# Program order for TensorE in the expert stage, merged slot products, and unread products between trunk and experts

## The chip, the cores and the metric

The kernel runs on one core of a Trainium2 chip. The metric is device time in microseconds (us) of one execution; the time of a kernel is the median of its runs. One execution was taken by the hardware profiler as well. The engines are named as in its rows: PE is TensorE (PEld its weight loads), DVE is VectorE, ACT is ScalarE, POOL is GpSimd, SP is SyncE, which issues most of the DMA transfers.

## The reference

A decoder of two layers over 512 tokens of width 1024, in fp32. Each layer has two attention branches, gates, an output projection, and a feed-forward part: dense in layer 0, and in layer 1 the mixture of experts, at which the change is aimed:

```python
D_MODEL, SEQ, DEPTH = 1024, 512, 2
N_EXPERTS, TOP_K, D_FF_EXPERT = 8, 2, 1408

def swiglu(h, w_gu, w_dn):
    gu = h @ w_gu
    g, u = jnp.split(gu, 2, axis=-1)
    return (jax.nn.silu(g) * u) @ w_dn

def moe_swiglu(h, w_router, w_gu_e, w_dn_e):
    """Top-2 of 8 SwiGLU experts; softmax over the selected router logits."""
    logits = (h @ w_router).astype(jnp.float32)
    top_val, top_idx = lax.top_k(logits, TOP_K)
    top_w = jax.nn.softmax(top_val, axis=-1)
    combine = jnp.sum(jax.nn.one_hot(top_idx, N_EXPERTS, dtype=jnp.float32) * top_w[..., None], axis=-2)
    combine = combine.astype(h.dtype)
    out = jnp.zeros_like(h)
    for e in range(N_EXPERTS):
        out = out + combine[..., e:e + 1] * swiglu(h, w_gu_e[e], w_dn_e[e])
    return out

def reference(...):
    for l in range(DEPTH):
        ...                                  # attention branches, gates
        x = x + (g_sb * y_sb + g_fx * y_fx) @ w_out[l]
        h = rmsnorm(x, g_ffn[l])
        if l % 2 == 0:
            x = x + swiglu(h, w_gu_dense[l // 2], w_dn_dense[l // 2])
        else:
            x = x + moe_swiglu(h, w_router[l // 2], w_gu_exp[l // 2], w_dn_exp[l // 2])
    return x
```

## The kernel before, in words

**Numbers.** An fp32 operand is split into a high part of type fp32r (a cast) and a low part (a subtraction), and a product of two operands is the sum of three products on PE: high by high, high by low, low by high. The weights of the experts come from memory as fp32 (`er`, by SP's queue, eleven raw buffers) and are split in the kernel: ACT makes `ehi` (L1467), DVE makes `elo` (L1468). `e_split` (L1455) does this for one piece, two pieces ahead of the product that reads it; the table `SN` says at which steps.

**From trunk to experts.** The last projection of the trunk (`out_proj1`, L1041) makes, half by half, the router logits (`half_logits`, L1070) and the two best experts of each token (`top2`, L1162). `route` (L1174) turns the choice into positions: where in its expert's list a token stands (products with triangular matrices, on PE). `moe` (L1705) then prepares the first expert. `prep_a` (L1485) compares the positions with a row of numbers (`one_hots`, L1268, tiles `oh`), multiplies the one-hots with token numbers (`slots`, L1278: 16 products of one column for 192 slots in two groups), casts the sums to an index `ix`, and issues the gather of the tokens' rows by POOL (an indirect DMA, 128 rows to `xg`, and under an If 64 more rows to a part of `ao`). The routing weights of the slots come from `slot_weights` (L1298, 8 products of three columns). `prep_b` (L1517) transposes the gathered rows on PE (L1526) and splits them into `xh` and `xl`; `prep_over` (L1532) does the same for the 64 further rows, into `aot`.

**An expert.** `expert_blocks` (L1551) has four gate/up blocks u of 352 + 352 columns, each of k = 0..7 with six products of 352 columns (L1646 gate, L1647 up), and then three blocks of the down projection with k = 0..10 and three products each (L1680 to L1682). A step is named (u, k); the down projection's are (4, k) to (6, k). After each block the result is activated (`am`), transposed, and split into `ah` and `al` (`tr`, L1567, L1581). Experts with more than 128 tokens (in these inputs the first and the fifth) run the further 64 rows as well: products under an If at the start of each block (L1626, over-products, into the two PSUM banks `mm`), folded by `ov_gu` (L1585: ACT copies, DVE adds, ACT's silu, DVE multiplies; `fold` is L1546), transposed by `ov_tr` (L1592, L1597, L1601), and multiplied with the down weights (L1694, L1695). The next expert is prepared meanwhile: `prep_a` at the steps `PA`, `PA1`, `PA2`, `prep_b` at `PB`, `PB1`, `prep_over` at `PO`; the rest of the first expert's preparation (`route_rest`, L1206: weights and a ranking of the experts by their counts) at `P0`. `OV`, `OV3` and `OT` are the k at which the folding and `ov_tr` stand.

**What sets the order.** ACT's instructions stand in the order in which the code issues them. Those of PE, DVE and POOL are put in order by a scheduler, by estimates and dependences, except where the code calls `keep_in_program_order`. In the trunk this holds for PE as well.

## Time and profile before

| | before |
|---|---|
| median of 3 runs | 1703.38 us (1703.5, 1700.21, 1703.38) |
| profiled execution | 1699.52 us |
| its span, first to last instruction | 1697.7 us |
| mean granted clock of PE | 0.992 |
| PE busy | 1634.0 us, 96% of the span |
| DVE / ACT / POOL busy | 64% / 58% / 12% |
| moved by DMA | 273.73 MB, 161 GB/s on average |

A row of the windows gives the busy time of each engine in a stretch, its number of instructions in brackets, the clock granted to PE as a share of full speed, the mean busy share of the 16 DMA engines, and what they moved. A row of the timeline gives the start, the busy time, engine, source line, operation, output and inputs by the program's names, the shape, and how many such instructions the row joins; in square brackets stand the idle time of the engine ahead of it and what released it. Ends of products are modelled and a product's row is longer than the distance to the next one, so the distance from start to start is what a product costs in a dense row of them. The trunk fills the span up to some 1183 us, the first expert's products begin at 1198.00 us, and the eighth expert ends at some 1685 us.

### The profile page before, as it was taken

How to read it: one execution, taken by the hardware profiler on the slowest of the kernel's cores; microseconds unless marked ns; L12 is line 12 of the kernel's file. 1: busy time of each engine (PE TensorE's matmuls, PEld its weight loads, DVE VectorE, ACT ScalarE, POOL GpSimd, SP SyncE). 2: the span in 40 equal slices, each digit the busy share in tenths (PEclk: the TensorE clock that was granted, in tenths of full speed). 3: DMA queues.
4: the chain of work that ended last, by engine and by line, in shares of the span. 5: the costliest groups of instructions: out<-in, count | busy, mean ns of one | idle time of the engine just before them, and what ended most of it. 6: DMA issues, size and time to landing. Idle time of an engine off the chain costs nothing. (4 is left out here: it accounts for less than half of the span.)

```text
span 1697.7 us, 26160 instructions
## 1 busy us (share of the span) xinstructions
PE 1634.0 (96%) x9031; PEld 1425.7 (84%) x9031; DVE 1093.7 (64%) x1844; ACT 977.9 (58%) x1750; POOL 205.5 (12%) x315
## 2 busy tenths in 40 slices
PE   6999999999999999999999999998899999999996
PEld 6878987888888888888878987887889999999996
DVE  5588678666533332336588688655767878767984
ACT  5677589755322222324677589643656776656873
POOL 6122000001000000100122000102012201102200
PEclk9999999999999999999999999999899999999998
DMA  7334332235333332443433233352959899869993
GB/s 181 108 96 116 82 88 71 86 110 165 100 98 99 100 99 84 134 130 100 112 105 107 72 88 78 110 194 95 311 201 331 296 360 351 295 209 336 321 344 87
DMA packets 270840, 273.73 MB, mean 161 GB/s; under 512 B 11424, under 2 KB 259232, under 8 KB 270688
## 3 DMA queue, kind: packets, MB, share of 16 engines
q1 hardware_dynamic: 255936, 230.98, 43.2%
q0 software_dynamic: 12288, 37.40, 8.1%
q10 hardware_dynamic: 2464, 3.41, 0.6%
q8 instruction: 85, 1.39, 0.3%
q14 instruction: 67, 0.55, 0.1%
HBM read 250.21 MB, written 13.14 MB: 155 GB/s over the span
## 5 line engine op out<-in xcount | busy, mean ns | idle before, releaser
L320 PE MATMUL mm<-b,whi 128*128 128x512 f32 x1072 | 426.7, 398 | 3.6 <-DVE b L534 2.7
L322 PE MATMUL mm<-b,wlo 128*128 128x512 f32 x1072 | 419.4, 391 | 0.0
L321 PE MATMUL mm<-b,whi 128*128 128x512 f32 x1072 | 419.4, 391 | 0.0
L297 DVE TENSOR_TENSOR wlo<-wr,whi 128x1024 fp32r<-128x1024 f32 (+1 forms) x176 | 213.3, 1213 | 214.5 <-ACT whi L296 212.5
L296 ACT CAST whi<-wr 128x1024 fp32r<-128x1024 f32 (+1 forms) x176 | 183.2, 1043 | 268.9 <-PE mm L321 121.5
L1468 DVE TENSOR_TENSOR elo<-er,ehi 128x1408 fp32r<-128x1408 f32 (+3 forms) x200 | 305.1, 1569 | 26.0 <-ACT ehi L1467 15.9
L1467 ACT CAST ehi<-er 128x1408 fp32r<-128x1408 f32 (+3 forms) x200 | 256.2, 1324 | 18.7 <-DMA er<-in_w_gu_exp_dram 6.2
L320 PEld LDWEIGHTS mm<-b,whi 128*128 128x128 f32 x1072 | 201.7, 188 | 45.4 <-DVE b L534 4.7
L322 PEld LDWEIGHTS mm<-b,wlo 128*128 128x128 f32 x1072 | 201.3, 188 | 42.8 <-DVE wlo L297 0.4
L321 PEld LDWEIGHTS mm<-b,whi 128*128 128x128 f32 x1072 | 201.7, 188 | 38.5 <-issue 0.2
L356 PE MATMUL mm<-whi,b 128*128 128x256 f32 x320 | 92.0, 288 | 1.8 <-DVE b L532 1.1
L357 PE MATMUL mm<-wlo,b 128*128 128x256 f32 x320 | 91.0, 285 | 0.4 <-DVE wlo L297 0.4
L358 PE MATMUL mm<-whi,b 128*128 128x256 f32 x320 | 90.8, 284 | 0.0
L1681 PE MATMUL pa<-elo,ah 128*128 128x352 f32 (+1 forms) x264 | 85.6, 324 | 2.7
L1682 PE MATMUL pa<-ehi,al 128*128 128x352 f32 (+1 forms) x264 | 84.4, 320 | 3.3 <-DVE al L1581 3.3
L1680 PE MATMUL pa<-ehi,ah 128*128 128x352 f32 (+1 forms) x264 | 86.2, 327 | 0.9
L1647 PE MATMUL pa<-elo,xh 128*128 128x352 f32 x256 | 83.7, 327 | 2.1 <-PEq L1620 0.5
L1646 PE MATMUL pa<-ehi,xh 128*128 128x352 f32 x256 | 85.7, 335 | 0.0
L1647 PE MATMUL pa<-ehi,xl 128*128 128x352 f32 x256 | 83.2, 325 | 0.9
L1646 PE MATMUL pa<-elo,xh 128*128 128x352 f32 x256 | 83.0, 324 | 0.3 <-DVE elo L1468 0.3
L1646 PE MATMUL pa<-ehi,xl 128*128 128x352 f32 x256 | 83.2, 325 | 0.0
L1647 PE MATMUL pa<-ehi,xh 128*128 128x352 f32 x256 | 82.9, 324 | 0.0
(351 smaller groups left out, 3087.7 us busy)
## 6 DMA issues: line engine op xcount, KB each, us to landing
er<-in_w_gu_exp_dram SPq DMA_DIRECT2D x248, 352.0 KB
wr<-in_w_in_dram SPq DMA_DIRECT2D x80, 512.0 KB
wr<-in_w_gu_dense_dram SPq DMA_DIRECT2D x44, 512.0 KB
er<-in_w_dn_exp_dram SPq DMA_DIRECT2D x32, 704.0 KB
wr<-in_w_dn_dense_dram SPq DMA_DIRECT2D x20, 512.0 KB
er<-in_w_dn_exp_dram SPq DMA_DIRECT2D x16, 640.0 KB
er<-in_w_dn_exp_dram SPq DMA_DIRECT2D x16, 528.0 KB
b<-b POOLq DMA_DIRECT2D x64, 128.0 KB, 2.8
```

Of the source, the lines that this page charges most:

```text
L296: self.nc.scalar.copy(hi, raw)
L297: self.nc.vector.tensor_sub(lo, raw, f32v(hi))
L320: self.nc.tensor.matmul(ps, hi[:, j], hh[j], start=st, stop=False)
L321: self.nc.tensor.matmul(ps, hi[:, j], hl[j], start=False, stop=False)
L322: self.nc.tensor.matmul(ps, lo[:, j], hh[j], start=False, stop=sp)
L356: nc.tensor.matmul(o, a, hi[:, j], start=first, stop=False, skip_group_check=True)
L357: nc.tensor.matmul(o, a, lo[:, j], start=False, stop=False, skip_group_check=True)
L358: nc.tensor.matmul(o, b, hi[:, j], start=False, stop=last, skip_group_check=True)
L1467: self.nc.scalar.copy(hi, raw)
L1468: self.last_dve = self.nc.vector.tensor_sub(lo, raw, f32v(hi))
L1646: nc.tensor.matmul(pg, x[:, k], w[:, 0, kk], start=s0, stop=s1)
L1647: nc.tensor.matmul(pu, x[:, k], w[:, 1, kk], start=s0, stop=s1)
```

## The change

- **Order on PE.** The call of `moe` stands in a context that keeps PE's instructions in program order, too. With it go changes of place: the over-products of a block (`mm_over`) are issued at the block's start, but for the first block of the first expert, where `prep_over` is issued at k = 2 and the over-products at k = 4; the folding `ov_gu` stands at k = 5 of each block (k = 7 in the first block of the first expert), that of the last gate/up block too, and `ov_tr` at k = 3 of the down projection, not 8.
- **Preparation.** `PA` becomes (2, 1), (2, 6), (3, 1) while the first expert runs, and (0, 6), (1, 5), (2, 4) in the others. `route_rest` is issued ahead of the first expert's blocks, its slot weights at the new `P0`, (2, 0) and (2, 2). The one-hots are all made on DVE.
- **Slot products.** In the seven later experts `slots_all` multiplies the one-hots with five columns at once: three of the weight and two of the token number, which POOL copies into `cols`. Eight products take the place of 16 and 8, and two sums on DVE take the place of a cast and a sum per group.
- **Unread products.** `busy(n)` issues n bf16 products of 384 columns, of constants, into a PSUM tile that nothing reads: 3 and 13 around the last logits, 4 in `route`, 28 after the first expert's slot products.

```diff
--- before.py
+++ after.py
@@ -44,14 +44,16 @@
 ER = 11
 EA = 4
 ORDER = (7, 3, 4, 5, 0, 6, 1, 2)
-P0 = (0, 2), (0, 6), (1, 1)
-OV, OV3, OT, OY = 5, 6, 8, (5, 8)
+P0 = (2, 0), (2, 2)
+EO = 2
+OV, OT, OY = 5, 3, (5, 8)
 ER0 = 3
 LA = 2
 SN = (2, 4, 6, 8), (2, 4, 6, 8), (2, 4, 6, 8), (2, 4, 6), (7, 8, 9, 10), (1, 4, 8), (1, 4, 8)
 TU, TE = 5, 6
 TD = 5
-PA, PA1, PA2, PB, PB1, PO = (1, 2), (2, 0), (2, 4), (4, 2), (4, 7), (5, 4)
+PA = ((2, 1), (2, 6), (3, 1)), ((0, 6), (1, 5), (2, 4))
+PB, PB1, PO = (4, 2), (4, 7), (5, 4)
 FD = 3
 PINH = ()
 BK = 0, 1, 2, 3, 4, 5, 6, 7
@@ -1081,6 +1083,9 @@
             if after:
                 after()
             yield
+            last = t == NT - 1 and c == 1
+            if last:
+                self.busy(3)
             for j in range(4):
                 q = slice(j * P, (j + 1) * P)
                 if t == NT - 1:
@@ -1090,6 +1095,8 @@
                     nc.tensor.matmul(pl[:64, t * P:(t + 1) * P], self.wr[:, 4 * c + j], p[:, q],
                                      start=t + c + j == 0 and p is xs[0], stop=c + j == 4 and p is xs[1],
                                      skip_group_check=True)
+            if last:
+                self.busy(13)
 
         def ev_b(t, ps):
             v = x[t][1]
@@ -1138,6 +1145,13 @@
                 yield
 
         self.run(self.proj_tok(2, mh, ml, ev_a), second_half())
+
+    def busy(self, n):
+
+        ps = self.psa()
+        v, w = self.ident.bitcast(BF16)[:, :P], self.iotas.bitcast(BF16)
+        for _ in range(n):
+            self.tc.keep_in_program_order(self.nc.tensor.matmul(ps[:, :2 * CAP], v, w, start=True, stop=True))
 
     def router_consts(self):
         nc, cp, q = self.nc, self.cp, self.nc.gpsimd
@@ -1189,6 +1203,7 @@
                              stop=j == 1, skip_group_check=True)
         for t in range(NT):
             nc.tensor.matmul(pc[:, 0:NE], self.onesb, mb[:, t * NE:(t + 1) * NE], start=t == 0, stop=t == NT - 1)
+        self.busy(4)
         a, b = rp.tile([P, NT, NE], F32, name="r_a"), rp.tile([P, NT, NE], F32, name="r_b")
         nc.vector.tensor_scalar(b, self.M, -1.0, 1.0, op0=ALU.mult, op1=ALU.add)
         nc.vector.tensor_mul(a, pr[:, 0:32].rearrange("p (t e) -> p t e", e=NE), self.M)
@@ -1221,7 +1236,9 @@
         nc.vector.tensor_tensor(self.M, self.M, over_e(e2), op=ALU.mult)
         nc.vector.tensor_add(self.wt, self.s1, self.M)
         self.rank()
-        self.cols = rp.tile([P, NT, NE, 3], BF16, name="cols")
+        self.cols = rp.tile([P, NT, NE, 5], BF16, name="cols")
+        for j in range(2):
+            nc.gpsimd.tensor_copy(self.cols[:, :, :, 3 + j], self.tokc[:, :, j:j + 1].to_broadcast([P, NT, NE]))
         self.weight_cols(self.cols, self.wtr, rp.tile([P, NT, NE], F32, name="wrem"))
 
     def rank(self):
@@ -1275,6 +1292,26 @@
             oh.append(o)
         return oh
 
+    def slots_all(self, n, oh, cols):
+
+        nc, ps, res = self.nc, self.psy(), []
+        for b in range(0, n, P):
+            m = min(P, n - b)
+            o = ps[:m, (b // P) * 8:(b // P) * 8 + 5]
+            for t in range(NT):
+                nc.tensor.matmul(o, oh[t][:, b:b + m], cols[:, t], start=t == 0, stop=t == NT - 1)
+            res.append([b, m] + [self.ex.tile([P, 1], d, tag=g, bufs=4, name=self.nm(g))[:m]
+                                 for d, g in ((I32, "ix"), (F32, "w"))])
+
+        def fin():
+            for b, m, ix, w in res:
+                o = ps[:m, (b // P) * 8:(b // P) * 8 + 5]
+                with nc.allow_low_precision(reason="whole numbers below 512"):
+                    nc.vector.tensor_reduce(ix, o[:, 3:5], axis=AX.X, op=ALU.add)
+                nc.vector.tensor_reduce(w, o[:, 0:3], axis=AX.X, op=ALU.add)
+
+        return res, fin
+
     def slots(self, n, oh):
 
         nc = self.nc
@@ -1486,12 +1523,11 @@
 
         nc, ex = self.nc, self.ex
         o = ORDER[e]
-        oh = self.one_hots(CAP, self.posr[:, :, o:o + 1] if e else self.pos[:, :, 0:1], nc.gpsimd if e else nc.vector)
+        oh = self.one_hots(CAP, self.posr[:, :, o:o + 1] if e else self.pos[:, :, 0:1], nc.vector)
         yield
-        sl, fin = self.slots(CAP, oh)
+        sl, fin = self.slots_all(CAP, oh, self.cols[:, :, o]) if e else self.slots(CAP, oh)
         self.sl = sl
         if e:
-            wfin = self.slot_weights(oh, sl, self.cols[:, :, o], self.psl)
             yield
         fin()
         g = self.g = [ex.tile([P, D], F32, tag="xg0", bufs=1, name=self.nm("xg")), self.views[-1]]
@@ -1510,9 +1546,9 @@
             yield
             self.route_rest()
             yield
-            wfin = self.slot_weights(oh, sl, self.cols[:, :, o])
-            yield
-        wfin()
+            wfin = self.slot_weights(oh, sl, self.cols[:, :, o, 0:3])
+            yield
+            wfin()
 
     def prep_b(self):
 
@@ -1605,18 +1641,7 @@
             self.fold(yo[:, c], ops[d][:, :c.stop - c.start], yo[:, c])
             nc.vector.tensor_scalar_mul(yo[:, c], yo[:, c], sl[1][3])
 
-        def evac_gu(u, pg, pu):
-            c = slice(u * GC, (u + 1) * GC)
-            nc.scalar.activation(a[:, c], pg, AF.Silu)
-            nc.vector.tensor_mul(a[:, c], a[:, c], pu)
-
-        def evac_y(d, py):
-            c = dcol(d)
-            nc.scalar.activation(y[:, c], py, AF.Copy, scale=sl[0][3])
-
-        last = None
-        for u in range(DFE // GC):
-            ws = self.e_next(KD // GK)
+        def mm_over():
             with self.over(e):
                 for k in range(KD):
                     hi, lo = ws[k // GK]
@@ -1624,14 +1649,34 @@
                     for w, s0, s1 in ((hi, st, False), (lo, False, sp)):
                         for g in range(2):
                             nc.tensor.matmul(og[g], xo[:, k], w[:, g, kk], start=s0, stop=s1)
+
+        def evac_gu(u, pg, pu):
+            c = slice(u * GC, (u + 1) * GC)
+            nc.scalar.activation(a[:, c], pg, AF.Silu)
+            nc.vector.tensor_mul(a[:, c], a[:, c], pu)
+
+        def evac_y(d, py):
+            c = dcol(d)
+            nc.scalar.activation(y[:, c], py, AF.Copy, scale=sl[0][3])
+
+        last = None
+        for u in range(DFE // GC):
+            ws = self.e_next(KD // GK)
+            if (e, u) != (0, 0):
+                mm_over()
             if u:
                 evac_gu(u - 1, *last)
             last = pg, pu = self.psa()[:, :GC], self.psa()[:, :GC]
             for k in range(KD):
                 yield u, k
+                if (e, u, k) == (0, 0, EO):
+                    xo = self.prep_over(0)
+                    self.e_splits(LA)
+                if (e, u, k) == (0, 0, EO + 2):
+                    mm_over()
                 if (u, k) == (0, ER0) and self.rest:
                     self.rest()
-                if k == OV and u < 3:
+                if k == (OV if e or u else KD - 1):
                     with self.over(e):
                         ov_gu(u)
                 if k == TU:
@@ -1660,9 +1705,6 @@
                     tr(KE)()
                 if k in SN[4 + d]:
                     self.e_split()
-                if d == 0 and k == OV3:
-                    with self.over(e):
-                        ov_gu(3)
                 if d == 0 and k == OT:
                     with self.over(e):
                         ov_tr()
@@ -1714,6 +1756,7 @@
         pa = self.prep_a(0)
         next(pa)
         next(pa)
+        self.busy(28)
         self.hold = True
         self.e_splits(3)
         pb = self.prep_b()
@@ -1725,18 +1768,21 @@
             self.e_load()
         self.hold = False
         next(pb)
-        xo = self.prep_over(0)
-        self.e_splits(1 + LA)
+        xo = None
+        self.e_splits(1)
+        next(pa)
+        p0 = pa
         for e in range(NE):
             sl = self.sl
             for u, k in self.expert_blocks(e, sl, self.xs, xo):
                 if e == 0 and (u, k) in P0:
-                    next(pa, None)
+                    next(p0, None)
                 if e + 1 == NE:
                     continue
-                if (u, k) == PA:
+                at = PA[min(e, 1)]
+                if (u, k) == at[0]:
                     pa = self.prep_a(e + 1)
-                if (u, k) in (PA, PA1, PA2):
+                if (u, k) in at:
                     next(pa, None)
                 if (u, k) == PB:
                     pb = self.prep_b()
@@ -1848,7 +1894,8 @@
                 self.route()
             with experts:
                 self.moe_pools(experts)
-                self.moe()
+                with tc.manual_schedule(engines={mybir.EngineType.PE}):
+                    self.moe()
                 with tc.issue_after(self.last_dve.ins):
                     self.overflow_list()
         with ExitStack() as experts:
```

The first of two places: PE in the first expert. `pa` are the banks of the main products, `mm` those of the over-products, `xh`/`xl` the gathered rows and `ehi`/`elo` the split weights; the rows stand in the middle of the second gate/up block before.

```order
L1646 MATMUL pa_12002<-ehi_11893,xl_11726 128x352
L1647 MATMUL pa_12003<-ehi_11893,xl_11726 128x352
L1646 MATMUL pa_12002<-ehi_11893,xh_11725 128x352
L1647 MATMUL pa_12003<-ehi_11893,xh_11725 128x352
L1646 MATMUL pa_12002<-elo_11894,xh_11725 128x352
L1620 COMPARE_AND_BRANCH
L1626 MATMUL mm_11660<-ehi_11790,aot 128x352
L1626 MATMUL mm_11661<-ehi_11790,aot 128x352
L1626 MATMUL mm_11660<-elo_11791,aot 128x352
```

The over-products (L1626) of block 1 come behind 33 of the 48 main products of the block, the last five of which are shown. After the change PE has this, at the end of block 0 and the start of block 1 (L1680 is the If of the folding, L1691 and L1692 are the main products, L1645 is the If of the over-products):

```order
L1680 COMPARE_AND_BRANCH
L1680 UNCONDITIONAL_BRANCH x2
L1691 MATMUL pa_11874<-ehi_11825,xh_11779 128x352
L1692 MATMUL pa_11875<-ehi_11825,xh_11779 128x352
L1691 MATMUL pa_11874<-elo_11826,xh_11779 128x352
L1692 MATMUL pa_11875<-elo_11826,xh_11779 128x352
L1691 MATMUL pa_11874<-ehi_11825,xl_11780 128x352
L1692 MATMUL pa_11875<-ehi_11825,xl_11780 128x352
L1645 COMPARE_AND_BRANCH
L1651 MATMUL mm_11685<-ehi_11903,aot 128x352
L1651 MATMUL mm_11686<-ehi_11903,aot 128x352
```

The over-products (L1651) moved to the head of the block, six main products behind the branch of the folding; the main products of block 1 now stand behind them.

The second place: DVE in the first expert's down projection before. The three rows between the branches fold the last over-block, `al` is the low part of the activations, `aot` that of the further rows.

```order
L1664 COMPARE_AND_BRANCH
L1549 TENSOR_TENSOR ao<-mm_11660,ao 64x352
L1549 TENSOR_TENSOR ao<-mm_11661,ao 64x352
L1590 TENSOR_TENSOR ao<-ao 64x352
L1664 UNCONDITIONAL_BRANCH x2
L1581 TENSOR_TENSOR al_11802<-py_12424,ah_11801 128x384
L1529 TENSOR_TENSOR xl_12407<-py_12443,xh_12406 128x512
L1667 COMPARE_AND_BRANCH
L1601 TENSOR_TENSOR aot<-py_12468,aot 128x8x64
L1601 TENSOR_TENSOR aot<-py_12479,aot 128x3x64
```

After the change, the folding of the last over-block (L1585, L1626) and what follows it:

```order
L1680 COMPARE_AND_BRANCH
L1585 TENSOR_TENSOR ao<-mm_11685,ao 64x352
L1585 TENSOR_TENSOR ao<-mm_11686,ao 64x352
L1626 TENSOR_TENSOR ao<-ao 64x352
L1680 UNCONDITIONAL_BRANCH x2
L1505 TENSOR_TENSOR elo_12427<-er_12063,ehi_12426 128x1408
L1617 TENSOR_TENSOR al_11873<-py_12413,ah_11872 128x384
L1656 TENSOR_TENSOR am<-am,pa_12339 128x352
L1565 TENSOR_TENSOR xl_12454<-py_12455,xh_12453 128x512
L1709 COMPARE_AND_BRANCH
L1637 TENSOR_TENSOR aot<-py_12466,aot 128x8x64
L1637 TENSOR_TENSOR aot<-py_12477,aot 128x3x64
```

The folding moved ahead of a split of weights (`elo`) and of both subtractions into `al`, and the two rows for `aot` ahead of the second of these.

## Rows read from the trace of the kernel before

**Rows 1.** The page's head; busy us, share of the span, instructions.

```profile
span 1697.7 us, 26160 instructions
...
PE 1634.0 (96%) x9031; PEld 1425.7 (84%) x9031; DVE 1093.7 (64%) x1844; ACT 977.9 (58%) x1750; POOL 205.5 (12%) x315
```

**Rows 2.** Windows: the stretch, its length, and the columns named above.

```profile
1184.00:1186.00 2.00, 0.96 (x8) 0.89 (x9) 1.21 (x7) 0.50 (x2) 0.00 (x0) 1.00 0.41 154
1186.00:1188.00 2.00, 0.26 (x5) 0.19 (x5) 1.99 (x12) 0.00 (x0) 1.00 (x2) 0.70 0.23 90
1192.00:1194.00 2.00, 0.00 (x0) 0.00 (x0) 2.00 (x2) 1.65 (x2) 1.63 (x2) 0.50 0.63 178
1202.00:1204.00 2.00, 2.00 (x9) 2.00 (x9) 1.42 (x2) 2.00 (x2) 0.00 (x0) 0.53 1.04 347
1204.00:1206.00 2.00, 2.00 (x14) 2.00 (x14) 2.00 (x2) 1.53 (x2) 0.00 (x0) 1.00 1.04 366
1350.00:1400.00 50.00, 48.64 (x320) 46.64 (x320) 41.19 (x39) 36.07 (x38) 7.28 (x6) 1.00 1.05 354
```

**Rows 3.** Timeline between trunk and first expert, DVE and PE.

```profile
1188.87 0.99 DVE L1273 TENSOR_SCALAR oh<-iotas,r_pos 128x192 bf16<-128x192 f32 x4
...
1189.22 1.41 PE L1288 MATMUL py<-tokc,oh 128*128 128x1 bf16 x16 [0.89 <-DVE oh L1273]
...
1196.21 1.97 PE L1526 MATMUL py<-ident,xg 128*128 128x128 f32 x8 [5.58 <-DMA xg<-hd,ix]
...
1198.00 0.66 PE L1646 MATMUL pa<-ehi,xh 128*128 128x352 f32 x1
...
1198.75 0.50 PE L1646 MATMUL pa<-elo,xh 128*128 128x352 f32 x1
...
1199.04 0.50 PE L1647 MATMUL pa<-elo,xh 128*128 128x352 f32 x1
...
1200.27 1.08 PE L1539 MATMUL py<-ident,ao 64*128 64x64 f32 x8 [0.73 <-DMA ao<-hd,ix]
...
1201.28 0.66 PE L1646 MATMUL pa<-ehi,xl 128*128 128x352 f32 x1
...
1203.80 0.36 PE L1646 MATMUL pa<-ehi,xh 128*128 128x352 f32 x1
```

**Rows 4.** Timeline of PE in the second expert, where the third is prepared.

```profile
1306.31 0.32 PE L1647 MATMUL pa<-ehi,xl 128*128 128x352 f32 x1
1306.47 0.69 PE L1288 MATMUL py<-tokc,oh 128*128 128x1 bf16 x16
1307.10 0.47 PE L1306 MATMUL py<-cols,oh 128*128 128x3 bf16 x8
1307.50 0.43 PE L1646 MATMUL pa<-ehi,xh 128*128 128x352 f32 x1
```

**Rows 5.** Timeline of PE: down projection of the first and the fifth expert.

```profile
1265.49 0.43 PE L1682 MATMUL pa<-ehi,al 128*128 128x352 f32 x1 [2.11 <-DVE al L1581]
...
1268.84 0.40 PE L1694 MATMUL mm<-ehi,aot 128*128 128x352 f32 x1 [0.95 <-DVE aot L1601]
...
1506.89 0.43 PE L1682 MATMUL pa<-ehi,al 128*128 128x352 f32 x1 [1.15 <-DVE al L1581]
...
1510.10 0.40 PE L1694 MATMUL mm<-ehi,aot 128*128 128x352 f32 x1 [0.79 <-DVE aot L1601]
```

**Rows 6.** Timeline of the first expert's first block, ACT and DVE.

```profile
1207.02 1.38 ACT L1467 CAST ehi<-er 128x1408 fp32r<-128x1408 f32 x1 [0.56 <-DMA er<-in_w_gu_exp_dram]
...
1208.99 1.38 ACT L1467 CAST ehi<-er 128x1408 fp32r<-128x1408 f32 x1 [0.59 <-DMA er<-in_w_gu_exp_dram]
...
1211.22 0.93 ACT L1548 COPY ao<-mm 64x352 f32<-64x352 f32 x2 [0.85 <-PE mm L1626]
...
1211.70 1.07 DVE L1549 TENSOR_TENSOR ao<-mm,ao 64x352 f32<-64x352 f32 x2 [1.43 <-ACT ao L1548]
```

**Rows 7.** Waits of PE from 1183 us: what, total us, times, longest.

```profile
PE py L1288 <- POOL oh L1273: 0.7, 2, 0.5
```

More of the change, by code (lines that the diff above doesn't have):

```diff
@@ L1606, in ov_y @@
             nc.vector.tensor_scalar_mul(yo[:, c], yo[:, c], sl[1][3])
+        def mm_over():
+            with self.over(e):
+                for k in range(KD):
+                    hi, lo = ws[k // GK]
+                    st, sp, kk = k == 0, k == KD - 1, k % GK
+                    for w, s0, s1 in ((hi, st, False), (lo, False, sp)):
+                        for g in range(2):
+                            nc.tensor.matmul(og[g], xo[:, k], w[:, g, kk], start=s0, stop=s1)
         def evac_gu(u, pg, pu):
@@ L1619, in expert_blocks @@
             ws = self.e_next(KD // GK)
-            with self.over(e):
-                for k in range(KD):
-                    hi, lo = ws[k // GK]
-                    st, sp, kk = k == 0, k == KD - 1, k % GK
-                    for w, s0, s1 in ((hi, st, False), (lo, False, sp)):
-                        for g in range(2):
-                            nc.tensor.matmul(og[g], xo[:, k], w[:, g, kk], start=s0, stop=s1)
+            if (e, u) != (0, 0):
+                mm_over()
             if u:
@@ L1662, in expert_blocks @@
                     self.e_split()
-                if d == 0 and k == OV3:
-                    with self.over(e):
-                        ov_gu(3)
                 if d == 0 and k == OT:
```

## The prediction

> **What bounds the kernel now.** I read the page first, then the stretches of equal length, then the timeline of the two stretches in which TensorE (PE) is not busy, then who waits for whom. The page shows PE busy for 96% of a span of 1697.7 us [rows 1], so only PE's own time and the holes in it count. The execution took 1699.52 us, 1.8 us more than its span; the median of the three runs is 1703.38, 3.9 above it, so I make the sum against the profiled execution and take it off the median.
>
> The first hole lies between the trunk and the first expert. PE is busy 0.96 and 0.26 of 2 us, and then the granted clock goes to 0.50, the 1.2 GHz level; it is back at 1.00 (2.4 GHz) only after some 1203.8, by which time the first expert has long begun [rows 2]. In the hole stand the slot products, a gather for which PE waits 5.58 us, eight transposes, and then twelve products of the first expert at a pitch of 0.29 us [rows 3], where a steady expert has 0.16 (the 1306.31 and 1306.47 rows of [rows 4]). Among them PE waits once more for the second gather, the rows beyond 128 (L1539).
>
> The experts themselves are dense. What the change touches there is the slot products, 24 in 1.03 us of a steady expert [rows 4], and four waits in the two experts with more than 128 tokens, the first and the fifth: PE waits for al and aot there [rows 5]. DVE is busy 41.2 of 50 us in steady experts and PE 48.6 [rows 2].
>
> **The change part by part.**
>
> *Unread products.* 48 products of 384 columns are added. At the high level one costs 384/352 of 0.16, 0.175 us. The three and the thirteen stand where PE waits for the last logits and for r_Mb, the four where it waits for the one-hots (0.89 us idle, [rows 3]); 13 x 0.175 = 2.3 us fits into the holes of the 1184 and 1186 rows of [rows 2], which leave 1.04 and 1.74 us, with little to spare. The 28 take 4.9 us and begin after the slot products, at about 1190.9, so they end near 1195.8; the gathered rows come at 1196.2, or a quarter us earlier (below). If they run over, the transposes wait: between 0 and 0.5 us, I take 0. What they can buy is the clock of the work behind them. Twelve first products took 3.85 us (four from 1198.00 to 0.29 behind 1199.04, eight from 1201.28 to 1203.80) and would take 1.92: 1.9 us. Four of the eight transposes stand before the first cast: 1.97/4, 0.5 us, less 0.05. The eight transposes of the second gather, 1.01 us from row to row, halve: 0.45. The sixteen slot products, 1.41 us, take 0.63 at the high level [rows 4], but the last one-hot ends at 1189.86 [rows 3], so only 0.25 is left. The wait for the second gather shrinks by 0.2, since twelve products stand before it now, not four. Together 3.25 us, if the clock holds.
>
> *Program order, the first block of the first expert.* Now the over-products of block 1 stand at its start and not in its middle, and the folding of block 0 (ov_gu, which reads the same two PSUM banks) only six products ahead of them; behind the waiting product all of PE is queued. PE would be there at 1197.3 + 80 x 0.16 + 0.75 for the gather + 0.55 for its transposes = 1211.4. On ACT the folding stands behind the split of the ninth piece of weights. The pieces come 2.0 us apart (the splits at 1207.02 and 1208.99 each waited for a DMA, [rows 6]), so the ninth comes at about 1211.0; the loads wait for the first cast, which is 0.7 earlier now, so 1210.3. The split takes 1.38, and from the start of ACT's two copies to the end of DVE's two adds it is 1.55 [rows 6]: the banks are free at 1213.2, or at 1212.7 for the first. PE waits 1.6 us here, a new wait that eats half of the 3.25. Its bounds are 0 (the piece comes two us sooner) and 3.25. I take 1.6: **1.65 us** are left.
>
> *Merged slot products.* Per prepared expert sixteen one-column products (0.63 us, 1306.47 to 1307.10) go and eight of three columns become eight of five. The eight cost 0.40 in [rows 4]; two columns more are nothing at that pitch. Seven experts are prepared this way: 7 x 0.63 = **4.4 us**. On DVE the sums take the place of two casts; the one-hots (0.99 us for four, [rows 3]) come from POOL to DVE, whose 8.8 idle us of 50 hide them. The lower bound of a saved product is the 0.03 to which the row's pitch can be rounded, 3.4 us in all; the upper is 0.05, the pitch of the three-column ones, 5.6.
> The Trainium skill, page "TensorE: Matmul & The Clock Gate", section "Wait — 56ns, not 53.3ns?", puts the floor from start to start at about 25 ns however small the product. The row differs from it, at 39 and 50 ns with a weight load before each product; by the page's floor the term would be an estimated 2.8 us and the whole sum 11.1.
>
> *Waits for one-hots.* In the first expert PE waited 0.7 us in two pieces for POOL's one-hots [rows 7]; with what a product's modelled end hides it is **1.0 us**. Now DVE makes them at (2,1) for products at (2,6), five k or 4.8 us later. Bounds 0 and 1.5; I take 1.0.
>
> *Folding in program order.* In both experts with over-products al stood behind the last folding on DVE, and the folding behind ACT's copies: PE waited 2.11 and 1.15 for al, 0.95 and 0.79 for aot [rows 5]. Each has 0.16 more, since a modelled product ends 0.32 behind its start and the next could start 0.16 behind it: 5.0 + 0.64 = 5.6 us. Now ov_gu(3) stands at block 3, k 5, some 4.8 us before ov_tr (three k of 0.96 us, three of 0.48 and the transposes between), and ov_tr at k 3 of the down projection, with al and aot three and eight k ahead of their readers. The folding takes some 1.6 us from its first copy to its last add [rows 6], so nothing of the wait is late next. Bounds: 0, if another wait of the same chain takes its place at ov_tr, and 5.6. I take **5.6**.
>
> *Nothing.* The If of the second gather, route_rest earlier on DVE (small operations in DVE's waits for the first split), two POOL copies into cols (POOL is idle), the skipped Ifs of the six other experts (the same number in both). If the cover of route_rest went, it would be its some 4 us of small operations in front of the pieces of block 1, and PE gets there at 1213; so it stays hidden.
>
> Sum: 1.65 + 4.4 + 1.0 + 5.6 = 12.65, say 12.7 us. The profiled execution would be 1686.8, the median 1703.4 - 12.7 = **1690.7 us**.
>
> **The rivals.**
>
> *The clock falls all the same.* For it: the slot products and route's products have few columns, and the stretches around 1188 to 1190.5 stay thin. Then the 28 run at 0.35, 9.8 us from 1190.9, and end at 1200.7 if no rise comes, 4.5 us past the rows' arrival, or at some 1199 if it rises on the way, as it did at 1203.8 among the first products [rows 2, 3]. The first products then start at 1200.3 to 1202. What is late hits the wait for the banks first, so the first term becomes +0.8 to -2.3: sum 11.9 to 8.7, time 1691.5 to 1695, say 1693.5. Against it: before the fall PE was busy 0.26 of 2 us, and there the added products stand now.
> The same page, section "What's actually happening", says that the moment of the rise shifts between runs of one kernel; by that rule this term would differ from run to run. No run here shows it.
>
> *The folding waits stay.* For it: ACT and DVE keep their order of splits, and ov_tr needs ao in order. Then 12.7 - 5.6 = 7.1 us: 1696.3.
>
> *Late one-hots make it slower.* In program order PE cannot put other products ahead of the slot products of the next expert at (1,5). DVE now makes the one-hots between splits of 1.6 us. If they come behind two more splits, PE waits 3.2 us in each of seven experts: 22.4 - 12.7 = 9.7 us slower, 1713. It decides from 1.8 us per expert on. For it: DVE is the next busiest, and PE did wait for one-hots in the first expert. Against: they are made from (0,6), seven k or 6.7 us ahead, and DVE has 8.8 us of 50 free.
>
> *The order changes nothing.* Waits of the sort of the first block's, one or two us in several places, cancel the gain to within 0.2%, about 3.4 us, which is what a measurement of this kernel can tell from no change: 1702.
>
> **How the numbers follow.** The forecast (a gain of 10.8 to 15.5): 0.47. The clock falls: 0.15. The folding waits stay, or half of them: 0.18. More than 15.5, without the new wait in the first block: 0.07. Cancelled: 0.08. Slower: 0.05. The first four are faster by over 0.2%: 0.87. The range: down to 1684.5 (12.7 + 1.6 of the new wait + the upper bounds 1.2 and 0.5, and the runs' own spread of 3 us), up to 1698.5, which takes in both cases of a smaller gain; outside are the slower end, cancellation, and a little below.
>
> **What would show it.** In the changed profile the clock rows of 1184 to 1204 all at 1.00 would show the first term right, and the first product at 1197.3; a wait of PE's over-product for DVE's ao at some 1211 to 1213 the new wait. From the third block of a steady expert's row: eight products of five columns in 0.4 us, and a period 0.6 shorter. No wait for al or aot in the first and fifth expert. Wrong would be: PE waiting for oh in several experts, for ao at L1633's transposes, or a clock of 0.50 behind 1190.

## The result, and the profile after

The changed kernel takes 1686.06 us (median of 4 runs, 1685.85 to 1688.47), the kernel before 1703.16 beside it: a ratio of 0.9907 [0.9889, 0.9924], 17.1 us less by the medians. (A ratio is taken over undisturbed runs of both kernels and can differ a little from that of the medians.) The profiled execution took 1686.10 us, 13.4 less than that of before.

The page's head and busy times, as [rows 1]:

```profile
span 1684.3 us, 26036 instructions
...
PE 1633.7 (97%) x8967; PEld 1423.1 (84%) x8967; DVE 1098.7 (65%) x1872; ACT 978.1 (58%) x1750; POOL 173.8 (10%) x289
```

PE's busy time is the same to 0.3 us, but it is not the same work: 48 products were added and 112 slot products went. Where the time went is read from the starts of the experts' first main products, here that of the second expert, before and after:

```profile
1290.13 0.32 PE L1646 MATMUL pa<-ehi,xh 128*128 128x352 f32 x1
```

```profile
1283.90 0.40 PE L1691 MATMUL pa<-ehi,xh 128*128 128x352 f32 x1
```

Up to the end of the first expert 6.2 us went, in the seven others 0.8, 1.0, 0.7, 2.8 (the fifth), 0.8, 0.7 and 0.1, and 0.3 behind the last product.

Windows of the stretch of [rows 2] (length; busy us of PE, PEld, DVE, ACT, POOL; granted clock; DMA):

```profile
1186.00:1188.00 2.00, 1.26 (x9) 0.74 (x8) 2.00 (x12) 0.00 (x0) 0.84 (x2) 1.00 0.15 57
1190.00:1192.00 2.00, 1.45 (x14) 0.87 (x14) 0.57 (x3) 2.00 (x2) 0.35 (x1) 0.67 0.30 52
1192.00:1194.00 2.00, 2.00 (x8) 0.93 (x7) 2.00 (x2) 1.79 (x2) 1.60 (x2) 0.50 0.67 196
1194.00:1196.00 2.00, 2.00 (x14) 1.21 (x13) 2.00 (x2) 0.00 (x0) 0.12 (x1) 0.98 0.88 325
1200.00:1202.00 2.00, 2.00 (x18) 1.71 (x17) 1.65 (x2) 0.79 (x3) 0.00 (x0) 1.00 1.01 335
1350.00:1400.00 50.00, 48.95 (x312) 46.91 (x310) 42.83 (x44) 36.43 (x37) 4.63 (x2) 1.00 1.05 355
```

The hole is filled and the clock fell all the same, but at 1190.7 us and for 3.4 us only, from just ahead of the 28 added products to the tenth of them (0.67 and 0.50), and not from 1186.8 to 1203.9 as before. When the first expert begins it is back at 1.00. In steady experts DVE is 1.6 us of 50 busier and POOL 2.7 less.

The timelines that answer to [rows 3, 6], of PE and then of all engines:

```profile
1191.12 6.17 PE L1154 MATMUL pa<-iotas,ident 128*128 128x384 bf16 x28 [0.52 <-issue]
1197.12 1.04 PE L1562 MATMUL py<-ident,xg 128*128 128x128 f32 x8
1198.40 0.43 PE L1691 MATMUL pa<-ehi,xh 128*128 128x352 f32 x1 [0.24 <-ACT xh L1564]
```

```profile
1210.92 1.38 ACT L1504 CAST ehi<-er 128x1408 fp32r<-128x1408 f32 x1 [0.63 <-DMA er<-in_w_gu_exp_dram]
...
1212.04 0.32 PE L1692 MATMUL pa<-ehi,xl 128*128 128x352 f32 x1
1212.32 0.92 ACT L1584 COPY ao<-mm 64x352 f32<-64x352 f32 x2
1212.80 1.07 DVE L1585 TENSOR_TENSOR ao<-mm,ao 64x352 f32<-64x352 f32 x2 [0.24 <-ACT ao L1584]
...
1213.46 0.40 PE L1651 MATMUL mm<-ehi,aot 128*128 128x352 f32 x1 [1.10 <-DVE ao L1585]
...
1214.01 0.40 PE L1651 MATMUL mm<-ehi,aot 128*128 128x352 f32 x1
```

The 28 products take 6.17 us, ten of them at the lower level (0.32 us each, then 0.16), and end 0.9 us behind the point where the gathered rows let PE start before (1196.21). So the first main product is 0.4 us later than before, not 0.7 earlier. Then comes the wait that was forecast: the split at 1210.92 stands on ACT ahead of the folding's copies, PE's first over-product of block 1 starts 1.42 us behind the product ahead of it (1212.04) and the next one waits again.

PE in the second expert, as [rows 4]: one row of eight products of five columns where 24 stood.

```profile
1296.84 0.47 PE L1302 MATMUL py<-cols,oh 128*128 128x5 bf16 x8
```

Waits of PE from 1183 us (what, total, times, longest), as [rows 5, 7]:

```profile
PE mm L1651 <- DVE ao L1585: 1.1, 1, 1.1
PE mm L1193 <- DVE r_Mb L1184: 0.8, 1, 0.8
PE py L1633 <- DVE xl L1565: 0.7, 2, 0.4
...
PE pa L1722 <- PEq L1572: 0.4, 1, 0.4
...
PE py L1325 <- DVE oh L1290: 0.2, 1, 0.2
```

The waits for al, aot and POOL's one-hots are gone; the largest that is left is the new one. At the transposes of the folded rows (L1633) PE waits 0.7 us in two pieces, put down to `xl` and not to `ao`.

### The profile page after: what moved, and what is told of

Its sections match the earlier page's. It is cut to its first block, busy times and chain, and to the rows that moved or that the text cites. A ratio compares the mean times of both kernels' runs of the same rounds, so it can differ in the third digit from the quotient of the medians.

```text
span 1684.3 us, 26036 instructions
## 1 busy us (share of the span) xinstructions
PE 1633.7 (97%) x8967; PEld 1423.1 (84%) x8967; DVE 1098.7 (65%) x1872; ACT 978.1 (58%) x1750; POOL 173.8 (10%) x289
## 5 line engine op out<-in xcount | busy, mean ns | idle before, releaser
L1691 PE MATMUL pa<-ehi,xh 128*128 128x352 f32 x256 | 86.9, 340 | 3.8 <-ACT xh L1564 0.2
L1691 PE MATMUL pa<-ehi,xl 128*128 128x352 f32 x256 | 82.7, 323 | 0.0
L1691 PE MATMUL pa<-elo,xh 128*128 128x352 f32 x256 | 82.6, 323 | 0.0
L1692 PE MATMUL pa<-ehi,xh 128*128 128x352 f32 x256 | 82.5, 322 | 0.0
L1692 PE MATMUL pa<-elo,xh 128*128 128x352 f32 x256 | 82.5, 322 | 0.0
L1692 PE MATMUL pa<-ehi,xl 128*128 128x352 f32 x256 | 82.3, 322 | 0.0
## 6 DMA issues: line engine op xcount, KB each, us to landing
er<-in_w_dn_exp_dram SPq DMA_DIRECT2D x32, 704.0 KB, 10.9
er<-in_w_dn_exp_dram SPq DMA_DIRECT2D x16, 640.0 KB, 10.4
er<-in_w_dn_exp_dram SPq DMA_DIRECT2D x16, 528.0 KB, 10.5
```

The source lines that it names most:

```text
L1691: nc.tensor.matmul(pg, x[:, k], w[:, 0, kk], start=s0, stop=s1)
L1692: nc.tensor.matmul(pu, x[:, k], w[:, 1, kk], start=s0, stop=s1)
```

## The experiments

Each line of the table was timed against the kernel before on the same chip; the span is that of its profiled execution. "b" is the kernel before with an edit, "a" the changed one.

| | median us | ratio to before | span |
|---|---|---|---|
| b_again | 1701.61 | 1.0002 [0.9993, 1.0011] | 1697.3 |
| b_busy | 1697.67 | 0.9984 [0.9974, 0.9993] | 1696.2 |
| b_fold | 1700.39 | 0.9999 [0.9990, 1.0008] | 1697.6 |
| a_again | 1686.64 | 0.9922 [0.9909, 0.9936] | 1683.8 |
| a_nobusy | 1686.42 | 0.9910 [0.9897, 0.9924] | 1684.5 |
| a_sched | 1689.85 | 0.9928 [0.9914, 0.9942] | 1688.0 |
| a_fold | 1690.72 | 0.9930 [0.9917, 0.9942] | 1688.1 |
| a_slots | 1692.85 | 0.9941 [0.9929, 0.9953] | 1688.7 |
| a_pool | 1696.70 | 0.9983 [0.9974, 0.9992] | 1694.8 |
| a_ov5 | 1685.22 | 0.9893 [0.9879, 0.9908] | 1684.2 |
| a_ov5_nobusy | 1685.07 | 0.9897 [0.9883, 0.9912] | 1683.0 |
| a_best | 1684.45 | 0.9905 [0.9890, 0.9920] | 1682.7 |

Sets on one chip: b_again, b_busy, a_nobusy, a_sched; a_fold, a_slots, a_ov5, a_ov5_nobusy; a_again, b_fold, a_pool, a_best. The kernel before has a median of 1701.47, 1703.75 and 1701.16 us in the three, so medians of different sets can differ by 2 us for that reason alone; each ratio is taken within its set.

### Why the median moved more than the profile: b_again and a_again

The two kernels unchanged.

> The kernel before, unchanged, to see the span and granted clock of its timed executions. Its profiled execution took 1699.52 us at a mean clock of 0.992, its timed runs had a median 3.6 us above. Theory A: the extra time is a longer stretch at the 1.2 GHz level between trunk and experts; 3.6 us of it would be some 7 us more at that level, so a mean clock of 0.990 in executions of some 1703 us and 0.992 in those of some 1700. Rival B: the extra time is elsewhere (transfers): 0.992 in both.

The timed runs do carry it in the clock: of 21 runs of before in that set the three of up to 1697.9 us of span show 0.991 or 0.992, the twelve of 1699.6 or more 0.987 to 0.989. But theory A's place is not what this trace shows. Windows of b_again's profiled execution, and PE in the first expert's down projection:

```profile
1198.00:1200.00 2.00, 1.82 (x12) 1.42 (x11) 1.27 (x2) 0.59 (x1) 0.00 (x0) 0.69 0.99 268
1200.00:1202.00 2.00, 2.00 (x16) 1.93 (x15) 0.69 (x1) 1.68 (x2) 0.00 (x0) 1.00 0.98 325
1264.00:1270.90 6.90, 6.32 (x28) 5.47 (x27) 4.47 (x5) 4.92 (x6) 0.00 (x0) 0.51 0.18 50
1270.90:1275.00 4.10, 4.10 (x27) 4.10 (x27) 3.15 (x3) 3.04 (x4) 0.00 (x0) 1.00 0.99 322
```

```profile
1263.28 0.43 PE L1682 MATMUL pa<-ehi,al 128*128 128x352 f32 x1 [2.12 <-DVE al L1581]
...
1267.27 0.63 PE L1694 MATMUL mm<-ehi,aot 128*128 128x352 f32 x1 [0.58 <-DVE aot L1601]
```

Here the clock came back at 1199.3 after the trunk, 4.6 us earlier than in the first profile, and block 0 took 14.61 us instead of 16.69. It fell a second time, from 1264.1 to 1270.9, behind the wait for al (2.12): the down projection's first block took 24.16 us instead of 21.87. The two cancel in this span. An execution with the late rise and the second fall would be 2.3 us above the first profile; a mean clock of 0.988 is some 41 us of 1700 at half, 26 in the first profile, so there is room for two such stretches of 6.8. Whether the timed runs have them, and where, no trace here shows.

> The changed kernel, unchanged, for its spread of spans and clocks beside the others of this set. Theory A (the extra time of the kernel before in its timed runs is a stretch at the 1.2 GHz level behind the folding waits, which the change removed): all runs within 1.5 us of 1685 to 1686, but for the trunk's own 1.1 us, mean clock 0.995 to 0.998, no low stretch between 1200 and 1675 us. Rival B (the spread comes from elsewhere): 3 us of spread here too.

There is no low stretch between 1194.1 and 1675.2 us in either of the changed kernel's two profiles. Of five runs three lie within 1.0 us (1685.69 to 1686.64), one at 1687.54 and one at 1689.89 with a clock of 0.994: rarer, not absent. From the lowest run to the lowest (1698.64 and 1685.69 in this set) the change gives 12.95 us, about as the profiles do; by the medians of this set it gives 14.5, where the first timing had 17.1.

### The unread products: b_busy and a_nobusy

```diff
 # b_busy: busy(3), busy(13), busy(4) at the same places, and in moe()
+        with self.tc.manual_schedule(engines={mybir.EngineType.PE}):
+            next(pa)
+            next(pa)
+            self.busy(28)
 # a_nobusy
     def busy(self, n):
+        return
```

> The kernel before with the 48 unread products alone (the first expert's slot products and the 28 behind them in program order on TensorE, nothing else moved). Theory A: the stretch at the 1.2 GHz level ends near 1194 us, not 1204; the first twelve products save 1.9 us, the transposes 0.9, the 28 products overrun the rows by 0.9: the profiled execution 2 us shorter, some 1697.5, and the median nearer to it, 1697 to 1699, a gain of 4 to 6. Rival B (the products do nothing here, the gain is order and slots): 1702 to 1704.

> The changed kernel without the 48 unread products. Theory A: the clock falls near 1187 us and comes back some 8 us behind the rows' arrival; in the profile the first block costs 2 us more and the new wait of 1.7 us ahead of block 1 is gone in part: 1687 to 1689, and the timed runs spread by 3 us as those of before do: median 1688 to 1691. Rival B (the clock is not worth anything, the overrun of 0.9 us goes): 1685 to 1686.

Windows of a_nobusy, and its waits:

```profile
1200.00:1202.00 2.00, 2.00 (x10) 1.61 (x8) 1.62 (x1) 0.08 (x1) 0.00 (x0) 0.50 1.05 354
1202.00:1204.00 2.00, 2.00 (x16) 1.93 (x16) 0.69 (x2) 1.31 (x2) 0.00 (x0) 0.93 1.01 346
```

```profile
PE py L1563 <- DMA xg<-hd,ix: 5.5, 1, 5.5
...
PE mm L1652 <- DVE ao L1586: 0.2, 1, 0.2
```

The clock was low until 1202.3, and the time is that of the changed kernel (a ratio of 0.9910; 0.9907 and 0.9922 with the products): the wait of PE ahead of block 1 is 0.2 there, not 1.1. To the end of the first two blocks (96 main and 64 over-products) the profiles give 1227.53 before, 1226.96 after, 1227.43 without the products. The clock alone does not decide it: in a_fold, below, which has the same first two blocks, the profile shows no low stretch here at all, and they end at 1227.45:

```profile
1191.27 4.72 PE L1154 MATMUL pa<-iotas,ident 128*128 128x384 bf16 x28 [0.48 <-issue]
...
1197.75 0.43 PE L1691 MATMUL pa<-ehi,xh 128*128 128x352 f32 x1 [0.24 <-ACT xh L1564]
...
1213.90 0.94 PE L1651 MATMUL mm<-ehi,aot 128*128 128x352 f32 x2 [2.19 <-DVE ao L1585]
```

PE came earlier and waited longer. In the six profiles with the folding of the first block at k = 7 in PE's program order (after, a_again, a_nobusy, a_fold, a_slots, a_pool) this over-product starts between 1213.00 and 1213.97, whatever the clock did. In the order of before the products are worth more: b_busy is through the same work at 1226.88, though its trunk ended 1.1 us later than that of before, 1.8 us in all, against the late rise. It has the folding waits of [rows 5] still, and four of its eleven runs lie at 1700.4 to 1701.6 with a clock of 0.991 to 0.993, seven at 1695.3 to 1698.0 with 0.994 to 0.996. So theory A holds for b_busy, and B, 0.4 over its range, for a_nobusy: what the clock gives is eaten by the next wait. An execution of the old order whose clock comes back early needs no unread products for it: that of b_again is through the same work at 1225.35, 1.6 us ahead of the changed kernel.

### The folding: a_fold, a_sched, b_fold

```diff
 # a_fold
-                if k == (OV if e or u else KD - 1):
+                if k == (OV if e or u else KD - 1) and u < 3:
...
-                if d == 0 and k == OT:
+                if d == 0 and k == 6:
+                    with self.over(e):
+                        ov_gu(3)
+                if d == 0 and k == 8:
 # a_sched
-                with tc.manual_schedule(engines={mybir.EngineType.PE}):
-                    self.moe()
+                self.moe()
 # b_fold: the kernel before with OT = 3 and ov_gu(3) at k = 5 of block 3
```

> The changed kernel with the folding of the last over-block back at k = 6 of the down projection and the transposes of the folded rows back at k = 8. Theory A (the place of the folding removed the waits for al and aot, and with them stretches at the 1.2 GHz level that follow such a wait in some executions): PE waits some 5 us again in the first and fifth expert, the profile at 1689 to 1691, timed runs up to 3 us more where the clock falls behind the wait (mean clock 0.994 or less in those), median 1691 to 1694. Rival B (TensorE's program order alone removed them): 1686 to 1687.5.

> The changed kernel with TensorE's order in the expert stage left to the scheduler again, everything else as changed. Theory A (the places of the folding in the code, which set the order of ACT, and the merged slots make the gain, TensorE's program order little): 1685 to 1688. Rival B (program order on TensorE itself removes the folding waits of 5.3 us and the waits for one-hots of 1 us): 1692 or more.

> The kernel before with the folding alone moved: ov_gu(3) to k = 5 of the last gate/up block, the transposes of the folded rows to k = 3. Theory A (the place removes the waits for al, the scheduler on TensorE keeps some waits for aot, as in the changed kernel with the scheduler): profile 2 to 4 us shorter, no stretch at the lower level in the first expert's down projection in most runs, so the median 4 to 6 us under the kernel before, 1696 to 1698. Rival B (without program order on TensorE the place does nothing): 1701 to 1703.

Waits of PE in a_fold, a_sched and b_fold, in this order:

```profile
PE py L1633 <- DVE al L1617: 3.1, 2, 1.6
PE mm L1651 <- DVE ao L1585: 2.2, 1, 2.2
...
PE mm L1739 <- DVE aot L1637: 0.5, 2, 0.2
```

```profile
PE py L1612 <- DVE aot L1637: 2.6, 2, 1.3
...
PE py L1575 <- DMA ao<-hd,ix: 1.6, 1, 1.6
```

```profile
PE py L1576 <- DVE aot L1601: 2.6, 2, 1.3
PE pa L1679 <- DVE al L1581: 2.3, 1, 2.3
```

With its old place (a_fold) the folding costs 1.5 us in the first expert's down projection and 1.6 in the fifth's, and no low stretch followed in the profile (PE waited 3.1 us in the two, not some 5); two of its five runs show a clock of 0.995 where the others have 0.998, and one of these is 2.0 us over the next. The profiled execution (1689.88) lies in theory A's range, the median 0.3 under it: the place is right, the price of the waits was 2 us too high. Moved alone under the scheduler (b_fold) it does nothing, as rival B said: the wait for al stays in the first expert (2.3), that for aot comes at PE's transposes (L1576, 2.6). With the new places but without program order (a_sched) the span is 3.7 us longer, between the two theories. The first block of the first expert's down projection takes 2.9 of it (21.32 us, 18.44 in the changed kernel): PE waits 1.3 for aot, and behind that wait the clock falls:

```profile
1261.04:1264.45 3.41, 3.41 (x15) 3.41 (x14) 2.10 (x3) 2.91 (x4) 0.00 (x0) 0.50 0.16 56
```

That of the fifth takes 0.7 more, with the same wait and no fall. The 1.6 us for the second gather cost nothing in the end: this down projection begins at 1253.88, 0.45 earlier than in the changed kernel. Neither half does it alone.

### The slot products: a_slots, and the one-hots: a_pool

```diff
 # a_slots
-        sl, fin = self.slots_all(CAP, oh, self.cols[:, :, o]) if e else self.slots(CAP, oh)
+        sl, fin = self.slots(CAP, oh)
         self.sl = sl
         if e:
+            wfin = self.slot_weights(oh, sl, self.cols[:, :, o, 0:3], self.psl)
             yield
         fin()
+        if e:
+            wfin()
 # a_pool
-        oh = self.one_hots(CAP, ..., nc.vector)
+        oh = self.one_hots(CAP, ..., nc.gpsimd if e else nc.vector)
```

> The changed kernel with the index and the weights of a slot by separate products again in the seven later experts (16 of one column and 8 of three, not 8 of five). Theory A: 0.6 us more in each of seven experts, in TensorE's row of the second block: 1690.2. Rival B (PE's products of few columns are hidden or cheaper, the term is half): 1688. Rival C (more: DVE or the gather becomes late too): 1692.

PE in the second expert, as in the changed kernel's row above:

```profile
1296.69 0.70 PE L1325 MATMUL py<-tokc,oh 128*128 128x1 bf16 x16
1297.32 0.47 PE L1343 MATMUL py<-cols,oh 128*128 128x3 bf16 x8
```

The block with the slot products is 0.61 to 0.64 us longer in each of the seven (9.36 for 8.75 us), the span 4.4: theory A's 1690.2 to 0.3 us in the profiled execution (1690.49). The median lies 2.4 above that, two of the six runs show a clock of 0.993 where the profile has 0.996, and the kernel before is some 2 us longer in this set than in the others, too; which of these makes the 2.4 stays open.

> The changed kernel with the one-hots of the later experts made by POOL again, not DVE. Theory A (they come late, and in program order TensorE waits in each expert): 0.5 to 1.8 us in each of seven, 1689 or more. Rival B (POOL has time: four take some 4.5 us there, and they are asked for 4.8 us ahead): 1685.5 to 1687, with at most one wait of 0.5 us.

Waits, timeline of the third expert (POOL) and windows of a_pool:

```profile
PE py L1302 <- POOL oh L1290: 5.3, 6, 1.2
```

```profile
1339.99 10.40 POOL L1290 TENSOR_SCALAR oh<-iotas,posr 128x192 bf16<-128x192 f32 x4
```

```profile
1344.00:1352.00 8.00, 6.25 (x43) 5.85 (x42) 6.22 (x10) 4.18 (x5) 7.07 (x4) 0.99 1.07 326
1352.00:1356.00 4.00, 3.85 (x15) 3.59 (x15) 2.69 (x3) 1.35 (x3) 1.75 (x1) 0.60 1.06 366
```

Four one-hots take POOL 10.40 us here; DVE makes four in 1.24 beside its splits in the changed kernel. PE's waits come to 5.3 us, in the third, fourth and seventh expert, and behind those of the first two of these the clock falls (0.60 in the second window): the block with them takes 12.5 us instead of 8.75, and 10.9 in the seventh, where it does not fall. The span grows by 10.5 us. Theory A's mechanism, in three experts and not seven, at twice its price.

### The new wait: a_ov5, a_ov5_nobusy, a_best

```diff
 # a_ov5, a_ov5_nobusy, a_best
-                if k == (OV if e or u else KD - 1):
+                if k == OV:
 # a_best, too
-        self.busy(28)
+        self.busy(22)
```

> The changed kernel with the folding of the first over-block of the first expert at k = 5, as in all other blocks, not 7, so that on ACT it stands ahead of the split of the ninth piece of weights. Theory A (the wait of 1.7 us ahead of block 1 is ACT's order): banks free 2 us earlier, the wait gone: 1684.4. Rival B (ACT's 4 us of copies, two table loads and silu push the splits, and block 1 or 2 waits for elo instead): 1686 or more.

> The same, and without the 48 unread products. Theory A (they were worth nothing since the wait ahead of block 1 took up what the clock gave): with the wait gone the lower clock of the first block costs about 2 us again: 1686 to 1686.5, that is 1.5 to 2 above the kernel with the folding at k = 5 and the products. Rival B (the first block is set by the pieces of weights, which come 2 us apart, whatever the clock): within 0.5 us of it.

> The changed kernel with the first folding at k = 5 and 22 unread products in place of 28 behind the first expert's slot products. Theory A: the wait of 1.7 us ahead of block 1 is gone and the transposes start with the rows, some 0.9 us earlier: 2.0 to 2.6 us under the changed kernel of this set, some 1683.5. Rival B (the first block is set by the weights' pieces, so the earlier start is lost): 1.0 to 1.7 us under it.

ACT in a_ov5: the ninth split (1215.44) now stands behind the folding.

```profile
1209.99 1.38 ACT L1504 CAST ehi<-er 128x1408 fp32r<-128x1408 f32 x1 [0.52 <-DMA er<-in_w_gu_exp_dram]
1211.39 0.92 ACT L1584 COPY ao<-mm 64x352 f32<-64x352 f32 x2
...
1215.44 2.65 ACT L1504 CAST ehi<-er 128x1408 fp32r<-128x1408 f32 x2
```

PE in a_best, and what is left of the wait:

```profile
1190.88 5.17 PE L1154 MATMUL pa<-iotas,ident 128*128 128x384 bf16 x22 [0.48 <-issue]
1195.88 1.04 PE L1562 MATMUL py<-ident,xg 128*128 128x128 f32 x8
1197.15 0.43 PE L1691 MATMUL pa<-ehi,xh 128*128 128x352 f32 x1 [0.24 <-ACT xh L1564]
```

```profile
PE mm L1651 <- DVE ao L1585: 0.2, 1, 0.2
```

In a_ov5 the first block takes 18.96 us, not 20.64: the wait of 1.7 was ACT's order. Of this the median shows 0.8 beside the first timing and the lowest run 1.6 (1684.29); in its profiled execution the trunk ended 1.2 us late, as in b_busy's, for a reason that stays open. Without the products (a_ov5_nobusy) the median is the same: its clock came back at 1199.6 that time, and the first block was 19.63 us but began 0.45 us earlier, since no product overruns the rows. Theory A falls there: the median is 0.15 from that of a_ov5, as rival B had it. With 22 products the transposes start at 1195.88, and a_best is 2.2 us under the changed kernel of its set by the medians and 1.1 by the spans; their intervals overlap, so it has the lowest median here, by a margin that these runs do not settle.

## Why the prediction was right, and where it was not

The forecast was 1690.7 us and 12.7 us of gain; the profiled executions differ by 13.4, the medians by 17.1 (14.5 when timed again). By the profiles the gain lies in the forecast of 10.8 to 15.5. By the medians of the first timing it lies above, in the case that had a chance of 0.07, "without the new wait in the first block"; that wait was there, so this is not how it came about. Step by step:

- **Merged slot products, 4.4 us forecast: right.** a_slots gives 0.61 to 0.64 us for each of seven, 4.4 in the span; the row's 39 ns a product were the price here. By the floor of 25 ns that the Trainium skill, page "TensorE: Matmul & The Clock Gate", section "Wait — 56ns, not 53.3ns?", states, it would have been an estimated 2.8. Products of route in the changed kernel do run 25 ns apart; what makes the difference was not tried.
- **Folding, 5.6: right in mechanism, 5.3 in size** (3.4 in the first block of the first expert's down projection, 1.9 in the fifth's). "In program order" and "at block 3, k 5" each proved necessary: b_fold and a_sched.
- **Unread products, 3.25, and the new wait, 1.6: the wait was right (1.3 and 0.4), the net of 1.65 was too high.** One step that failed is "they end near 1195.8": the clock had fallen as they began, as the rival had it, and they ended at 1197.1, so the first product came at 1198.4 and not at 1197.3. The other is the price of the new wait, 1.6 as if it were fixed: where the clock held (a_fold) the products ended at 1196.0 and the first product came at 1197.75, and the wait took that back, with 2.51 us from start to start. The forecast let the ninth piece come 0.7 earlier, with the first cast, and its split start at 1210.3; in the changed kernel it starts at 1210.92, in a_fold at 1211.27. The net to the end of the first two blocks was 0.6, and a_nobusy finds nothing in the ratio for all 48 products.
- **Waits for one-hots, 1.0: too low.** The third block, in which they and the slot products stood, took 15.89 before and 13.80 after; less the slots' 0.6 that leaves 1.5, the bound given. What of it is DVE's one-hots and what the new steps of the preparation was not tried apart. The point was larger than the term says: in program order one-hots left on POOL cost 10 us (a_pool), the rival's mechanism, at half of its price and in three experts. Moving them to DVE is what kept it away.
- **Not in the sum:** 0.1 to 0.4 us in each later expert beside the terms above, 1.2 together, and 0.3 at the end; no run here says what they are.
- **"I take it off the median": wrong by 4.4 us in the first timing, 1.8 in the second.** The profiled execution of before (1699.52) was shorter than all four runs timed beside the changed kernel. The term for the folding waits left out that behind such a wait the clock can fall, which cost 2.3 us for a stretch of 6.8 in one execution (b_again); how much of the medians' excess this makes is not shown. The moment of the rise moved, too: the clock came back after the trunk at 1203.9 and at 1199.3 in two executions of one kernel. The rule that the Trainium skill states on the same page, section "What's actually happening", that this moment shifts between runs, is borne out in kind; the page has 500 ns either way, and these two lie 4.6 us apart.

The terms as measured come to 0.6 + 4.4 + 5.3 + 1.5 + 1.2 + 0.3 = 13.3 of the 13.4. The one that was too high and those that were too low or missing lie on opposite sides; that the sum came within a microsecond of the profile is in that part luck.

## What to carry to other kernels

A saving that ends at an engine's next wait is worth only what is left of it: find the next wait first (here ACT's order of a split and a copy), and price the two together. A place in the code and a scheduler's freedom have to be changed together where a chain runs over three engines. A stall of two microseconds on TensorE can cost four: the clock fell behind waits of 2.12 us (b_again), 1.30 (a_sched) and 1.75 in two pieces (a_pool), and not behind one of 2.11 in the first profile of the kernel before. Look at several executions' granted clocks before a sum is set against a median.

## What the runs showed that was not expected

POOL took 10.4 us for four comparisons of 128x192 with which DVE is done in 1.24, in a stretch where both ran; over the kernel one took it 0.75 to 3.5 us. The trunk's last products came some 1.2 us later than in the first profile in two of fourteen profiled executions (b_busy, a_ov5) and 0.6 earlier in two (a_again, a_pool), for a reason that stays open. And in a_fold's profile the clock stayed up through the 28 unread products, while in the changed kernel's two it had fallen as they began.
